# Down projection of a decoder block: another order of the seven products, sums of weights made with their operand, six entries ahead

## The chip, the cores and the metric

One core of a Trainium2 chip runs the whole block in one launch. The metric is device microseconds from start to end of an execution; several executions are timed and the median is given. Another execution is recorded by the hardware profiler; its events are what "the profile" and "the trace" mean below.

## The reference

A decoder block on x of shape (1, 1024, 1024), float32: two mixers (a chunkwise mLSTM with four heads, and a causal pooling over four windows), gated and merged into the residual, then a SwiGLU feed-forward layer with 2816 hidden features and a last normalization. The change touches the final lines alone:

```python
x = x + (g_a * y_a + g_b * y_b) @ w_out[l]
h2 = rms_norm(x, norm2_g[l])
x = x + (jax.nn.silu(h2 @ w_ffn_gate[l]) * (h2 @ w_ffn_up[l])) @ w_ffn_down[l]
return rms_norm(x, final_norm_g)
```

## The kernel before

Everything is kept with features on partitions and tokens along a row. A float32 operand is split into a high and a low fp32r half (`split`, L130: ScalarE casts the high half, L131, and VectorE subtracts for the low one, L132), and a product of two such operands is three matmuls (`mm3`, L143 to L145). Large products use a scheme with seven half-size products instead of eight; the seven are named in `OPS` (b11, d1, d2, b21, d3, b22, d4), after the right-hand operand. The left operand of each is a block of weights or a sum of blocks.

The feed-forward stage makes the hidden features two tiles at a time (`hidden`, L840) and writes the seven right-hand operands of each of the 11 pairs to memory (`stage`, L834, DMA at L838, tensor `tg_d`). The names `fd`, `s` are its own operands, `e` its results.

The down stage (from L887) multiplies them with `w_down`. The 11 pairs are cut into three chunks of 4, 3 and 4 pairs. The work is a list of **entries** (L941): for each chunk c, each step s (one of the seven products), each of the four pairs of output rows q. One entry is a product over the chunk's pairs: 12 (or 9) matmuls of 128x512. TensorE gets the entries in this order, as the scheduler allows. Four pools lie at the right end of on-chip memory: `s1p` (sums of weights), `rbp` (second half of the raw weights), `tgp` (right-hand tiles `tg`, 13 places), `ap` (left operands `a`, 6 places). A pool that opens where another has closed lies over its tiles, and a load into it waits until those were last read.

The steps are in the same order in all chunks:

```python
STEPS = ("b21", "d1", "b22", "b11", "d2", "d3", "d4")
```

`down_lefts` (L903) is a generator for one (c, q): each `next` makes the left operand of the next step. At d1 it makes all sums of the weights at once (L920 to L924). `make_ready` (L943) draws the operand of the entry `EARLY` = 4 places ahead. `down_rights` (L935) issues on SP the `tg` loads of the next step when a step begins. `down_weights` (L896) loads raw weights: those of the next chunk at steps b22 (first halves) and d3 (second halves). Ahead of the loop SP gets the first weights, the `tg` of step one, the `rb` halves, the eight residual tiles `x` (L970), then the `tg` of step two.

A product is added to the residual by VectorE (L1037). b22 goes on in d1's PSUM bank (`C`), and d2, d3, d4 go on in b11's (`A`). PSUM has six banks `mm` and two `aux`.

In the last chunk the final normalization runs beside the products: `square` (L976) adds up squares, `scaled` (L984) applies the gain to the first 512 tokens, `turn` (L988) transposes those back to token rows, and `later_tokens` (L997) finishes the other 512 tokens: sums by token (L280), the power on POOL (L261), the factors spread along rows (L272 to L274), eight scalings on VectorE (L1004), eight stores. It is called after d3's last entry. The loop breaks off at the last entry (d4, q = 3), which is done in two halves of 256 tokens in the tail (L1057 to L1089), each followed by its mean (L1073), its power (L1074), transposes (L1077), scalings (L1086, L1088) and stores (L1089).

Of the kernel before, what the change touches and what calls it, by code (L numbers as in the profile page):

```python
# [47 lines left out]
EARLY = 4  # L48
# [18 lines left out]
def tile_hybrid_block(ctx, tc, x, xt, consts, params, w_fm, w_v, w_pool, w_a, w_b, w_out, w_gate, w_up, w_down, out, out_rows):  # L67
# [704 lines left out]
    with ExitStack() as c5:  # L772
# [116 lines left out]
        s1p = pool(c7, "s1p", KH, "right")  # L889
        rbp = pool(c7, "rbp", KH, "right")  # L890
        tgp = pool(c7, "tgp", 13, "right")
        ap = pool(c7, "ap", 6, "right")
        STEPS = ("b21", "d1", "b22", "b11", "d2", "d3", "d4")
        raws, lefts, rights, todo = {}, {}, {}, []
# [8 lines left out]
        def down_lefts(c, q):  # L903

            a11, a12 = raws[c, q, 0]
            n = a11.shape[-1]

            def tile_():
                t = ap.tile([P, 2, 512], F32R, tag="a", name="a")
                return t[:, :, :n]  # L910

            def op(src):
                t = tile_()
                operand(t, src)
                return t

            yield op(a12)
            a21, a22 = raws[c, q, 1]
            s1 = s1p.tile([P, 512], F32, tag="s1", name="s1")[:, :n]
            nc.vector.tensor_add(out=s1, in0=a21, in1=a22)  # L920
            t = op(s1)
            nc.vector.tensor_sub(out=a21, in0=a11, in1=a21)
            nc.vector.tensor_sub(out=s1, in0=s1, in1=a11)
            nc.vector.tensor_sub(out=a12, in0=a12, in1=s1)  # L924
            yield t
            yield op(a12)
            yield op(a11)
            yield op(s1)
            yield op(a21)
            t = tile_()  # L930
            nc.scalar.activation(out=t[:, 0, :], in_=a22, func=AF.Copy, scale=-1.0)
            nc.vector.scalar_tensor_tensor(out=t[:, 1, :], in0=a22, scalar=-1.0, in1=t[:, 0, :].bitcast(F32), op0=ALU.mult, op1=ALU.subtract)
            yield t

        def down_rights(c, s):  # L935
            for i in range(*CHUNKS[c]):
                t = tgp.tile([P, 2, 512], F32R, tag="tg", name="tg")
                nc.sync.dma_start(out=t.bitcast(F32), in_=tg_d[i, OPS.index(STEPS[s])].rearrange("p (a n) -> p a n", a=2))
                rights.setdefault((c, s), []).append(t)

        entries = [(c, s, q) for c in range(len(CHUNKS)) for s in range(len(STEPS)) for q in range(KH)]  # L941

        def make_ready(e):  # L943
            if e >= len(entries):
                return
            c, s, q = entries[e]
            if s == 0:
                lefts[c, q] = down_lefts(c, q)
            todo.append(next(lefts[c, q]))
# [23 lines left out]
    LAST = KT - 1  # L973
# [37 lines left out]
    A, C = [None] * KH, [None] * KH  # L1011
    whole = slice(0, 512)
    for e, (c, s, q) in enumerate(entries):
        final = c == len(CHUNKS) - 1
        if q == 0:
            if s + 1 < len(STEPS):
# [4 lines left out]
        if s == 2 and not final:  # L1021
            down_weights(c + 1, q, 0)
        if s == 5 and not final:
            down_weights(c + 1, q, 1)
        a, ts = todo.pop(0), rights[c, s]
        (o10, o11), (o20, o21) = halves(x3[q]), halves(x3[q + KH])
        if final and s == 6 and q == KH - 1:
            break
        if s == 0:
            ps = bank()  # L1030
        elif s in (1, 2):
            ps = C[q] = bank() if s == 1 else C[q]
        else:
            ps = A[q] = bank() if s == 3 else A[q]
        product(ps, a, ts, whole, s in (0, 1, 3), True)
        o = (o10, o21, o11, o10, o11, o21, o20)[s]
        nc.vector.tensor_add(out=o, in0=ps, in1=o)  # L1037
        if not final:
            continue
        if s == 3:  # L1040
            square(q, 0)
            scaled(q)
        if s == 4:
            square(q, 1)
            if q == 1:
                for t in range(4):
                    turn(t, 0, KH)
        if s == 5:
            square(q + KH, 1)
            if q == KH - 1:  # L1050

# [98 lines left out]
```

## Time and profile before

| what | value |
|---|---|
| median of 3 runs | 1507.25 us (1505.81 to 1508.13) |
| the profiled execution itself | 1509.98 us |
| its span in the trace | 1508.3 us |
| mean granted clock of TensorE | 0.99 of full speed |
| busy share of the span: TensorE, VectorE, ScalarE | 98%, 75%, 48% |
| bytes moved by DMA | 262.18 MB, mean 174 GB/s |
| down stage, from its first to its last product | 1267.5 to about 1489 us |

The span is what the trace shows; the execution's own time is a little longer. Busy shares are averages over stages with different limits, so the stretches around the change are read one by one. PE is TensorE, PEld its weight loads, DVE VectorE, ACT ScalarE, SP the engine that issues most DMAs (SPq is its DMA queue).

### The profile page before, as it was taken

Reading aid. Unit: us, or ns where it says so; the run is one execution under the profiler, and the core shown is the slowest. Engines: PE = TensorE matmul, PEld = TensorE weight load, DVE = VectorE, ACT = ScalarE, POOL = GpSimd, SP = SyncE. Lnnn points to the kernel's source line nnn. Section 1 sums busy time; section 2 is a strip of 40 time slices with the busy share of each in tenths; the row PEclk is TensorE's granted clock in tenths of the full one; section 3 lists DMA queues with packets and bytes.
Section 4 is the critical chain, followed back from the end, with each engine's and each line's share of the span. In section 5 each row is a group of like instructions: output and inputs, shape, how many; then the busy total and the mean of one; then the engine's idle time right before and its main releaser. Section 6 shows DMA issues by size and latency. Waiting matters only on the chain.

```text
span 1508.3 us, 19546 instructions
## 1 busy us (share of the span) xinstructions
PE 1480.2 (98%) x7051; PEld 1249.0 (83%) x7051; DVE 1130.9 (75%) x2033; ACT 729.3 (48%) x1327; POOL 28.5 (2%) x58
## 2 busy tenths in 40 slices
PE   9999999999999999999999999999999998899996
PEld 9998888878887789998888788888888887788885
DVE  5757878797877678766567779888888876666765
ACT  6475655556543478862233455444444442222243
POOL 0000000000000011110000000000000000000000
PEclk9999999999999999999999999999999999899998
DMA  6662433233333598728343326434444446966633
GB/s 204 198 248 86 151 126 126 98 140 112 140 105 119 176 314 290 247 78 303 129 127 124 105 82 232 168 140 155 156 150 154 158 150 258 407 246 250 240 148 112
DMA packets 101296, 262.18 MB, mean 174 GB/s; under 512 B 9804, under 2 KB 45772, under 8 KB 101200
## 3 DMA queue, kind: packets, MB, share of 16 engines
q1 hardware_dynamic: 86032, 221.09, 42.0%
q10 hardware_dynamic: 15168, 39.85, 7.0%
q8 instruction: 55, 0.90, 0.3%
q14 instruction: 41, 0.34, 0.1%
HBM read 172.29 MB, written 88.62 MB: 173 GB/s over the span
## 4 chain that ended last, share of the span: by engine, by line
PE 95%; DVE 2%; DMA 1%; issue 1%; ACT 0%; SPq 0%; POOLq 0%; POOL 0%; ACTq 0%; DVEq 0%
PE mm L143 26%; PE mm L145 26%; PE mm L144 26%; PE mm L155 14%; DMA v<-v_d 1%; PE aux L683 0%; PE mm L524 0%; DMA yb<-yb_d 0%; DVE x L1004 0%; PE aux L573 0%; DMA o<-in_xt 0%; DVE a L132 0%; PE aux L280 0%; PE mm L993 0%; PE aux L143 0%
## 5 line engine op out<-in xcount | busy, mean ns | idle before, releaser
L131 ACT CAST s<-raw 128x512 fp32r<-128x512 f32 x220 | 133.6, 621 | 194.4 <-PE mm L145 158.7
L132 DVE TENSOR_TENSOR s<-raw,s 128x512 fp32r<-128x512 f32 x220 | 148.6, 686 | 29.6 <-ACT s L131 29.0
L143 PE MATMUL mm<-fd,s 128*128 128x512 f32 x352 | 137.6, 392 | 3.0 <-ACT e L226 2.2
L143 PE MATMUL mm<-zd,s 128*128 128x512 f32 x352 | 137.6, 393 | 0.3 <-DVE o L234 0.3
L144 PE MATMUL mm<-fd,s 128*128 128x512 f32 x352 | 137.6, 391 | 0.0
L145 PE MATMUL mm<-fd,s 128*128 128x512 f32 x352 | 137.5, 391 | 0.0
L145 PE MATMUL mm<-zd,s 128*128 128x512 f32 x352 | 137.5, 391 | 0.0
L144 PE MATMUL mm<-zd,s 128*128 128x512 f32 x352 | 137.3, 390 | 0.0
L143 PE MATMUL mm<-tg,a 128*128 128x512 f32 (+1 forms) x312 | 122.3, 392 | 7.4 <-ACT a L131 7.4
L144 PE MATMUL mm<-tg,a 128*128 128x512 f32 (+1 forms) x312 | 121.7, 390 | 0.0
L145 PE MATMUL mm<-tg,a 128*128 128x512 f32 (+1 forms) x312 | 121.6, 390 | 0.0
L1037 DVE TENSOR_TENSOR x<-mm,x 128x512 f32<-128x512 f32 x83 | 57.2, 689 | 63.0 <-PE mm L145 62.9
L143 PE MATMUL mm<-zb,s 128*128 128x512 f32 x264 | 104.0, 395 | 0.0
L143 PE MATMUL mm<-fb,s 128*128 128x512 f32 x264 | 103.0, 391 | 0.0
L144 PE MATMUL mm<-fb,s 128*128 128x512 f32 x264 | 103.0, 390 | 0.0
L144 PE MATMUL mm<-zb,s 128*128 128x512 f32 x264 | 102.9, 390 | 0.0
L145 PE MATMUL mm<-zb,s 128*128 128x512 f32 x264 | 102.9, 390 | 0.0
L145 PE MATMUL mm<-fb,s 128*128 128x512 f32 x264 | 102.7, 390 | 0.0
L143 PEld LDWEIGHTS mm<-fd,s 128*128 128x128 f32 x352 | 66.3, 188 | 17.8 <-ACT e L226 2.9
L143 PEld LDWEIGHTS mm<-zd,s 128*128 128x128 f32 x352 | 66.1, 188 | 14.7 <-DVE o L234 0.8
L145 PEld LDWEIGHTS mm<-fd,s 128*128 128x128 f32 x352 | 66.4, 189 | 13.9
L144 PEld LDWEIGHTS mm<-zd,s 128*128 128x128 f32 x352 | 66.1, 188 | 14.1 <-issue 0.5
(330 smaller groups left out, 3445.3 us busy)
## 6 DMA issues: line engine op xcount, KB each, us to landing
tg_d<-t SPq DMA_DIRECT2D x77, 512.0 KB, 3.4
tg<-tg_d SPq DMA_DIRECT2D x77, 512.0 KB, 6.0
raw<-in_w_fm SPq DMA_DIRECT2D x44, 512.0 KB, 3.7
z_d<-o ACTq DMA_DIRECT2D x24, 512.0 KB, 2.9
raw<-in_w_gate SPq DMA_DIRECT2D x22, 512.0 KB, 3.7
raw<-in_w_up SPq DMA_DIRECT2D x22, 512.0 KB, 4.6
q_d<-x ACTq DMA_DIRECT2D x16, 512.0 KB, 2.7
rc<-z_d SPq DMA_DIRECT2D x32, 256.0 KB, 5.2
```

What stands on the lines that cost most here:

```text
L131: hi_made = nc.scalar.copy(out=hi, in_=src)
L132: split.last = hi_made.ins, nc.vector.tensor_sub(out=lo, in0=src, in1=hi.bitcast(F32)).ins
L143: nc.tensor.matmul(out, lhsT=l[0], rhs=r[0], start=start, stop=False, skip_group_check=resume)
L144: nc.tensor.matmul(out, lhsT=l[0], rhs=r[1], start=False, stop=False, skip_group_check=resume)
L145: mm3.last = nc.tensor.matmul(out, lhsT=l[1], rhs=r[0], start=False, stop=stop, skip_group_check=resume)
L155: nc.tensor.matmul(ps[half], lhsT=l[a], rhs=r[half][b], start=(k == 0 and (a, b) == (0, 0)), stop=(k == nk - 1 and a == 1),)
L1037: nc.vector.tensor_add(out=o, in0=ps, in1=o)
```

## The change

- `EARLY` is 6 instead of 4, `ap` has 8 places instead of 6, `tgp` 11 instead of 13; a pool `s4p` of two tiles is new, and the pools stand in another order (`tgp` ahead of `rbp`).
- The steps are b21, b11, d1, b22, d2, d3, d4 in the first two chunks; in the last chunk b21 comes last.
- `down_left` makes the operand of one entry with the sum that it needs: a21+a22 at d1, that less a11 and a12 less the result at b22, a11-a21 at d3. a12 is no longer overwritten.
- d1 and b22 have a bank each, `aux` for odd q and `mm` for even; d1's product is added in two places.
- Both halves of the next chunk's weights are loaded at d3.
- `later_tokens` still follows d3's last entry, which now is eight entries ahead of the end instead of four, since d4 and b21 follow it. The first 512 tokens of the rows 4 to 7 are turned at b21, q = 1; those of the rows 0 to 3 in the tail. The last entry is b21, q = 3, and the tail stores the columns from 512 on first.

```diff
 NPAIR = NFF // 2
 CHUNKS = ((0, 4), (4, 7), (7, 11))
 
-EARLY = 4
+EARLY = 6
 
 
 C_ID, C_TRI, C_ONE, C_INV = 0, 128, 256, 384
...
         c7 = ctx.enter_context(ExitStack())
         del places[0]
         s1p = pool(c7, "s1p", KH, "right")
+        s4p = pool(c7, "s4p", 2, "right")
+        tgp = pool(c7, "tgp", 11, "right")
         rbp = pool(c7, "rbp", KH, "right")
-        tgp = pool(c7, "tgp", 13, "right")
-        ap = pool(c7, "ap", 6, "right")
-        STEPS = ("b21", "d1", "b22", "b11", "d2", "d3", "d4")
-        raws, lefts, rights, todo = {}, {}, {}, []
+        ap = pool(c7, "ap", EARLY + 2, "right")
+
+        STEPS = [("b21", "b11", "d1", "b22", "d2", "d3", "d4")] * 2 + [("b11", "d1", "b22", "d2", "d3", "d4", "b21")]
+        raws, sums, rights, todo = {}, {}, {}, []
 
         def down_weights(c, q, fh):
             k0, k1 = CHUNKS[c]
...
             nc.sync.dma_start(out=t[:, :2 * n], in_=w_down[q, fh, :, 2 * k0 * P:2 * k1 * P])
             raws[c, q, fh] = t[:, :n], t[:, n:2 * n]
 
-        def down_lefts(c, q):
-
-            a11, a12 = raws[c, q, 0]
+        def down_left(c, s, q):
+
+            (a11, a12), (a21, a22) = (raws[c, q, fh] for fh in range(2))
             n = a11.shape[-1]
-
-            def tile_():
-                t = ap.tile([P, 2, 512], F32R, tag="a", name="a")
-                return t[:, :, :n]
-
-            def op(src):
-                t = tile_()
-                operand(t, src)
+            b = STEPS[c][s]
+            t = ap.tile([P, 2, 512], F32R, tag="a", name="a")[:, :, :n]
+            if b == "d4":
+                nc.scalar.activation(out=t[:, 0, :], in_=a22, func=AF.Copy, scale=-1.0)
+                nc.vector.scalar_tensor_tensor(out=t[:, 1, :], in0=a22, scalar=-1.0, in1=t[:, 0, :].bitcast(F32), op0=ALU.mult, op1=ALU.subtract)
                 return t
-
-            yield op(a12)
-            a21, a22 = raws[c, q, 1]
-            s1 = s1p.tile([P, 512], F32, tag="s1", name="s1")[:, :n]
-            nc.vector.tensor_add(out=s1, in0=a21, in1=a22)
-            t = op(s1)
-            nc.vector.tensor_sub(out=a21, in0=a11, in1=a21)
-            nc.vector.tensor_sub(out=s1, in0=s1, in1=a11)
-            nc.vector.tensor_sub(out=a12, in0=a12, in1=s1)
-            yield t
-            yield op(a12)
-            yield op(a11)
-            yield op(s1)
-            yield op(a21)
-            t = tile_()
-            nc.scalar.activation(out=t[:, 0, :], in_=a22, func=AF.Copy, scale=-1.0)
-            nc.vector.scalar_tensor_tensor(out=t[:, 1, :], in0=a22, scalar=-1.0, in1=t[:, 0, :].bitcast(F32), op0=ALU.mult, op1=ALU.subtract)
-            yield t
+            if b == "d1":
+                s1 = sums[c, q] = s1p.tile([P, 512], F32, tag="s1", name="s1")[:, :n]
+                nc.vector.tensor_add(out=s1, in0=a21, in1=a22)
+            elif b == "b22":
+                s1 = sums[c, q]
+                nc.vector.tensor_sub(out=s1, in0=s1, in1=a11)
+                s4 = s4p.tile([P, 512], F32, tag="s4", name="s4")[:, :n]
+                nc.vector.tensor_sub(out=s4, in0=a12, in1=s1)
+            elif b == "d3":
+                nc.vector.tensor_sub(out=a21, in0=a11, in1=a21)
+            operand(t, {"b21": a12, "b11": a11, "d1": sums.get((c, q)), "b22": b == "b22" and s4, "d2": sums.get((c, q)), "d3": a21}[b])
+            return t
 
         def down_rights(c, s):
             for i in range(*CHUNKS[c]):
                 t = tgp.tile([P, 2, 512], F32R, tag="tg", name="tg")
-                nc.sync.dma_start(out=t.bitcast(F32), in_=tg_d[i, OPS.index(STEPS[s])].rearrange("p (a n) -> p a n", a=2))
+                nc.sync.dma_start(out=t.bitcast(F32), in_=tg_d[i, OPS.index(STEPS[c][s])].rearrange("p (a n) -> p a n", a=2))
                 rights.setdefault((c, s), []).append(t)
 
-        entries = [(c, s, q) for c in range(len(CHUNKS)) for s in range(len(STEPS)) for q in range(KH)]
+        entries = [(c, s, q) for c in range(len(CHUNKS)) for s in range(len(OPS)) for q in range(KH)]
 
         def make_ready(e):
             if e >= len(entries):
                 return
-            c, s, q = entries[e]
-            if s == 0:
-                lefts[c, q] = down_lefts(c, q)
-            todo.append(next(lefts[c, q]))
+            todo.append(down_left(*entries[e]))
 
         early_made = []
         for q in range(KH):
...
         nc.sync.dma_start(out=t, in_=x2_d[j])
         x3.append(t)
     rows = [op.tile([P, D], F32, tag="o", name="o") for _ in range(4)]
-    LAST = KT - 1
+    LAST = KH - 1
     acc = [None, None]
 
     def square(j, half):
...
         for kp, t in enumerate(ts):
             mm3(ps, [a[:, i, kp * P:(kp + 1) * P] for i in range(2)], [t[:, i, sl] for i in range(2)], start and kp == 0, stop and kp == len(ts) - 1, True)
 
-    A, C = [None] * KH, [None] * KH
+    A = [None] * KH
     whole = slice(0, 512)
     for e, (c, s, q) in enumerate(entries):
         final = c == len(CHUNKS) - 1
         if q == 0:
-            if s + 1 < len(STEPS):
+            if s + 1 < len(OPS):
                 down_rights(c, s + 1)
             elif not final:
                 down_rights(c + 1, 0)
         make_ready(e + EARLY)
-        if s == 2 and not final:
-            down_weights(c + 1, q, 0)
-        if s == 5 and not final:
-            down_weights(c + 1, q, 1)
+        b = STEPS[c][s]
+        if b == "d3" and not final:
+            for fh in range(2):
+                down_weights(c + 1, q, fh)
         a, ts = todo.pop(0), rights[c, s]
         (o10, o11), (o20, o21) = halves(x3[q]), halves(x3[q + KH])
-        if final and s == 6 and q == KH - 1:
+        if final and b == "b21" and q == KH - 1:
             break
-        if s == 0:
-            ps = bank()
-        elif s in (1, 2):
-            ps = C[q] = bank() if s == 1 else C[q]
+        if b in ("b21", "d1", "b22"):
+            ps = bank("aux" if q % 2 else "mm")
         else:
-            ps = A[q] = bank() if s == 3 else A[q]
-        product(ps, a, ts, whole, s in (0, 1, 3), True)
-        o = (o10, o21, o11, o10, o11, o21, o20)[s]
-        nc.vector.tensor_add(out=o, in0=ps, in1=o)
+            ps = A[q] = bank() if b == "b11" else A[q]
+        product(ps, a, ts, whole, b in ("b21", "b11", "d1", "b22"), True)
+        for o in {"b21": [o10], "b11": [o10], "d1": [o21, o11], "b22": [o11], "d2": [o11], "d3": [o21], "d4": [o20]}[b]:
+            nc.vector.tensor_add(out=o, in0=ps, in1=o)
         if not final:
             continue
-        if s == 3:
+        if b == "d2":
+            square(q, 1)
+        if b == "d3":
+            square(q + KH, 1)
+            if q == KH - 1:
+                later_tokens()
+        if b == "d4":
+            square(q + KH, 0)
+            scaled(q + KH)
+        if b == "b21":
             square(q, 0)
             scaled(q)
-        if s == 4:
-            square(q, 1)
             if q == 1:
                 for t in range(4):
-                    turn(t, 0, KH)
-        if s == 5:
-            square(q + KH, 1)
-            if q == KH - 1:
-
-                nc.vector.tensor_add(out=o20, in0=ps, in1=o20)
-                later_tokens()
-        if s == 6:
-            square(q + KH, 0)
-            scaled(q + KH)
-    r, left, right = o20, a, ts
+                    turn(t, KH, KT)
+    r, left, right = o10, a, ts
     sq = sqd.tile([P, 512], F32, tag="sq1", name="sq")
     ms = sm.tile([P, 4], F32, tag="ms", name="ms")
     rs = sm.tile([P, 4], F32, tag="rs", name="rs3")
...
         product(ps, left, right, sl, True, True)
         if p == 0:
             for t in range(4):
-                turn(t, KH, LAST)
+                turn(t, 0, LAST)
             nc.vector.tensor_scalar(out=ms, in0=token_sums(acc[0], 4), scalar1=1.0 / D, scalar2=EPS, op0=ALU.mult, op1=ALU.add)
         nc.vector.tensor_add(out=r[:, sl], in0=ps, in1=r[:, sl])
         nc.scalar.activation(out=sq[:, sl], in_=r[:, sl], func=AF.Square)
...
         ps = bank("aux")
         for i in range(2):
             nc.tensor.transpose(out=ps[:, i * P:(i + 1) * P], in_=r[:, (2 * p + i) * P:(2 * p + i + 1) * P], identity=ident)
-        for c0, c1 in ((0, 512), (512, D)):
+        for c0, c1 in ((512, D), (0, 512)):
             for i in range(2):
                 t = 2 * p + i
-                sources = [(c0, min(c1, LAST * P), rows[t])] + [(LAST * P, D, ps)] * (c1 == D)
+                sources = [(c0, c1, rows[t])] if c0 else [(c0, LAST * P, rows[t]), (LAST * P, c1, ps)]
                 for a, b, src in sources:
                     o = rows[t][:, a:b]
                     src = ps[:, i * P:(i + 1) * P] if src is ps else o
```

The new line numbers that matter: `tg` loads L931, weight loads L902, `x` loads L960, additions L1025, squares L969 and L971, turned rows L983 and L985, the later tokens' scalings L994, tail L1055 to L1075.

The first place where the order moves is SP at the start of the down stage: from the first `tg` load of b21 to the first of the eight `x` loads. The names in brackets are the semaphores that an issue waits for (DMAHW: an earlier transfer, PE: TensorE). Before:

```order
L938 DMA tg<-tg_d 128x1024 [waits DMAHW0_49,PE_49]
L938 DMA tg<-tg_d 128x1024 [waits DMAHW1_49,PE_49]
L938 DMA tg<-tg_d 128x1024 [waits DMAHW2_49]
L938 DMA tg<-tg_d 128x1024 [waits DMAHW3_49,PE_49]
L900 DMA rb<-in_w_down 128x1024 [waits DMAHW4_49]
L900 DMA rb<-in_w_down 128x1024 [waits DMAHW5_49,PE_49]
L900 DMA rb<-in_w_down 128x1024 [waits DMAHW6_49]
L900 DMA rb<-in_w_down 128x1024 [waits DMAHW7_49]
L970 DMA x_11342<-x_d 128x1024 [waits DMAHW0_49]
```

With the change:

```order
L931 DMA tg<-tg_d 128x1024 [waits DMAHW0_49,PE_49]
L931 DMA tg<-tg_d 128x1024 [waits DMAHW1_49,PE_49]
L931 DMA tg<-tg_d 128x1024 [waits DMAHW2_49]
L931 DMA tg<-tg_d 128x1024 [waits DMAHW3_49]
L902 DMA rb<-in_w_down 128x1024 [waits DMAHW4_49]
L902 DMA rb<-in_w_down 128x1024 [waits DMAHW5_49]
L902 DMA rb<-in_w_down 128x1024 [waits DMAHW6_49]
L902 DMA rb<-in_w_down 128x1024 [waits DMAHW7_49]
L960 DMA x_11351<-x_d 128x1024 [waits DMAHW0_49]
```

The loads stand in the same order; the fourth `tg` and the second `rb` no longer wait for TensorE, the first and the second `tg` still do. Seven more `x` loads and then the `tg` of step two follow in both.

The second place is VectorE behind the additions of the last products (`x_…` are residual tiles, `rsb` the later tokens' factors, `o` the turned rows). Before:

```order
L1070 TENSOR_TENSOR x_11356<-mm,x_11356 128x256
L1069 TENSOR_SCALAR ms<-aux 128x4
L1072 TENSOR_SCALAR x_11356<-x_11356,par 128x256
L995 COPY o<-mm 128x384 x2
L1004 SCALAR_TENSOR_TENSOR x_11342<-x_11342,par,rsb 128x512
L1004 SCALAR_TENSOR_TENSOR x_11344<-x_11344,par,rsb 128x512
```

With the change:

```order
L994 SCALAR_TENSOR_TENSOR x_11363<-x_11363,par,rsb 128x512
L994 SCALAR_TENSOR_TENSOR x_11365<-x_11365,par,rsb 128x512
L985 COPY o<-mm 128x512
L971 TENSOR_TENSOR sq<-sq 128x512
L985 COPY o<-mm 128x512
L1025 TENSOR_TENSOR x_11355<-mm,x_11355 128x512
L1056 TENSOR_TENSOR x_11357<-mm,x_11357 128x256
```

Before, the eight scalings stood behind the last addition of all; now they stand ahead of the copies of turned rows, of the third product's addition (L1025) and of the last product's two (L1056).

## Rows read from the trace of the kernel before

**Rows 1.** The page, chain that ended last: shares of the span by engine

```profile
PE 95%; DVE 2%; DMA 1%; issue 1%; ACT 0%; SPq 0%; POOLq 0%; POOL 0%; ACTq 0%; DVEq 0%
```

**Rows 2.** Waits of PE from 1100 us: who waited, for whom; total, times, longest us

```profile
PE mm L143 <- ACT a L131: 7.4, 1, 7.4
```

**Rows 3.** Windows: us, busy of PE, PEld, DVE, ACT, POOL; PEclk, DMA share, GB/s

```profile
1280.00:1284.00 4.00, 0.00 (x0) 0.00 (x0) 4.00 (x8) 0.62 (x1) 0.00 (x0) 0.68 1.03 410
1284.00:1288.00 4.00, 2.06 (x5) 1.70 (x6) 4.00 (x8) 0.62 (x1) 0.00 (x0) 0.50 1.00 365
1288.00:1292.00 4.00, 4.00 (x11) 3.09 (x11) 1.95 (x4) 0.62 (x1) 0.00 (x0) 0.54 1.03 421
```

**Rows 4.** Timeline around the gap: start, duration in us, instruction, [idle before, releaser]

```profile
1265.87 0.39 PE L145 MATMUL mm<-fd,s 128*128 128x512 f32 x1
...
1266.55 0.39 PE L145 MATMUL mm<-fd,s 128*128 128x512 f32 x1
...
1275.52 0.68 DVE L132 TENSOR_TENSOR a<-s,a 128x512 fp32r<-128x512 f32 x1
...
1285.94 0.77 PE L143 MATMUL mm<-tg,a 128*128 128x512 f32 x1 [7.44 <-ACT a L131]
```

**Rows 5.** Timeline of SP's DMA issues at the start of the down stage

```profile
1258.65 4.84 SPq L938 DMA_DIRECT2D tg<-tg_d  x4
1263.55 4.71 SPq L900 DMA_DIRECT2D rb<-in_w_down  x4
1268.31 6.33 SPq L970 DMA_DIRECT2D x<-x_d  x8
1275.60 2.88 SPq L938 DMA_DIRECT2D tg<-tg_d  x3
```

**Rows 6.** DMA issues at 1267.83 and at 1275.60: count, KB, us to landing

```profile
rb<-in_w_down SPq DMA_DIRECT2D x1, 512.0 KB, 6.5
...
tg<-tg_d SPq DMA_DIRECT2D x1, 512.0 KB, 10.2
```

**Rows 7.** Timeline of SP, one step's tiles loaded with nothing else under way

```profile
1420.16 2.36 SPq L938 DMA_DIRECT2D tg<-tg_d  x4
```

**Rows 8.** DMA issues of that step: the first, and the fourth at 1422.20

```profile
tg<-tg_d SPq DMA_DIRECT2D x1, 512.0 KB, 3.2
...
tg<-tg_d SPq DMA_DIRECT2D x1, 512.0 KB, 6.3
```

**Rows 9.** Timeline of the tail, from 1481 us to the last power

```profile
1481.00 0.39 PE L143 MATMUL mm<-tg,a 128*128 128x512 f32 x1
...
1484.86 0.95 PE L280 MATMUL aux<-cst,sq 128*128 128x1 f32 x8
...
1487.38 0.28 PE L143 MATMUL mm<-tg,a 128*128 128x256 f32 x1
...
1492.66 0.58 ACT L274 COPY rsb<-aux 128x512 f32<-128x512 f32 x1 [0.48 <-PE aux L273]
...
1493.71 5.38 DVE L1004 SCALAR_TENSOR_TENSOR x<-x,par,rsb 128x512 f32<-128x512 f32 x8
...
1501.18 0.69 POOL L1074 TENSOR_TENSOR rs<-ms,nhalf 128x2 f32<-128x2 f32 x1 [1.25 <-DVE ms L1073]
```

**Rows 10.** Timeline of PE: eight transposes and the matmul behind them

```profile
1460.10 1.04 PE L993 MATMUL mm<-cst,x 128*128 128x128 f32 x8
1460.89 0.49 PE L143 MATMUL mm<-tg,a 128*128 128x512 f32 x1
```

**Rows 11.** Windows, columns as in 3: an idle stretch and what followed

```profile
851.00:853.00 2.00, 0.12 (x1) 0.00 (x0) 2.00 (x4) 1.09 (x3) 0.00 (x0) 1.00 0.00 0
855.00:858.00 3.00, 3.00 (x9) 2.33 (x8) 1.57 (x4) 0.75 (x2) 0.00 (x0) 0.50 1.00 376
```

**Rows 12.** Windows and lines of DVE: the full stretch

```profile
1290.00:1480.00 190.00, 190.00 (x844) 157.42 (x843) 122.20 (x198) 56.41 (x95) 0.00 (x0) 1.00 0.64 240
...
L1037 DVE TENSOR_TENSOR x<-mm,x 128x512 f32<-128x512 f32 x76 | 52.4, 690 | 60.2 <-PE mm L145 60.2
```

## The prediction

> **What bounds the kernel now.** I read the shares of the chain of waits first: TensorE carries 95% of the chain that ends last [rows 1], so an edit counts only where it moves a stretch in which TensorE stands still, or work that stands on TensorE. The waits of TensorE from 1100 us on come next: one of 7.4 us, before a matmul of the down stage [rows 2]. From 1290 to 1480 us TensorE is busy 190.00 of 190.00 us with 844 matmuls [rows 12], so a product of twelve matmuls takes 12 × 0.225 = 2.7 us there. That leaves three places for this change: the gap at the start of the down stage, the work that it puts on or takes off the full stretch, and the tail behind 1481 us.
>
> **The gap, and who really ends it.** b21 of chunk 0 ends at 1278.5 us, and d1 starts at 1285.94 [rows 4]. The profile puts the 7.44 us down to a ScalarE cast. That cast is not it: the low half of d1's first operand was finished by VectorE at 1275.52 + 0.68 = 1276.2 us [rows 4]. What landed last is the first tile of d1's right side: issued at 1275.60 [rows 5], 10.2 us to landing [rows 6], so 1285.8. It stood in line. SP issues four `tg`, four `rb`, eight `x` tiles and only then this one [rows 5]. The fourth `rb` (issued at 1267.83, 6.5 us [rows 6]) landed at 1274.3, and from there nine transfers of 512 KB took 11.5 us: 1.28 us each, with the DMA engines' share at 1.0 and 365 to 421 GB/s [rows 3]. The gap is a transfer limit, and it also brings the granted clock down: 0.68 in 1280 to 1284, 0.50 in 1284 to 1288, 0.54 in 1288 to 1292 [rows 3], about 5.7 us of work at the lower level (1.2 GHz), worth 2.8 us.
>
> By row the rate is 410 GB/s. The Trainium skill ("Perfetto Trace Analysis", Roofline) gives 358 GB/s as a core's share of memory and about 435 GB/s as what the 16 DMA engines of a single active core reach. As an estimate by that page a tile would cost 1.46 or 1.2 us, and the next part's term +5.2 or +4.1 us; the measured row decides.
>
> **Part 1, the new pools at the start.** Step two is now b11 instead of d1, but SP's order is the same: its tiles stand behind `tg` ×4, `rb` ×4, `x` ×8. So neither the six entries ahead nor the later sums (VectorE work) can close the gap: cost and gain nothing, covered by the queue of transfers. What does change is where the tiles lie. In the built order, before, the second and fourth `tg` and the second `rb` wait for TensorE; now the second `tg` does, and no `rb`. By the new places of the pools the second `tg` lies over the second of the four right-hand tiles of the last FFN product (d4), so it waits for that product's sixth matmul, which ends at 1265.87 + 0.39 = 1266.3 us [rows 4]. Before, all four `tg` were issued by 1263.5 [rows 5], and the `rb` that waited (for the same product's third tile, ninth matmul) could go at 1266.55 + 0.39 = 1266.9 [rows 4]. All 15 issues behind the second `tg`, up to b11's first tile, are queued behind that wait. At 1266.3 sixteen transfers are then to do (3 `tg`, 4 `rb`, 8 `x`, b11's first). From an idle start the nearest row is the step whose tiles were issued from 1420.16 on [rows 7]: the first took 3.2 us and the fourth, issued at 1422.20, 6.3 [rows 8], so the fourth lands 8.3 us after the first issue. 1266.3 + 8.3 + 12 × 1.28 = 1290.0 against 1285.8: **+4.2 us**. Bounds: if all after the first land at the full rate, 1266.3 + 3.2 + 15 × 1.28 = 1288.7 (+2.9); by counting that four transfers fewer are done (5.1 us) and the queue restarts 0.7 us earlier than at the `rb`, +4.4. I take the middle one since it uses the start-up as it was seen. b21 itself starts on time: its second tile lands by 1271 at the latest by the same rows, and is wanted about 1270, so up to 1 us of this may be lost earlier and is then hidden in the same gap. The half-clock stretch behind the gap stays as long as it is: 0.
>
> **Part 2, the full stretch.** Products: 84 before and after, 0. Added: twelve DVE additions (d1 into two places), 12 × 0.69 = 8.3 us [rows 12], and one less of that length (the extra addition at the end); VectorE is busy 122.2 of 190 us there [rows 12] and each bank is asked for again four entries (11 us) later, so 0; uncovered it would be TensorE waiting for a bank, at most the 8.3. `tgp` with 11 tiles instead of 13: the fourth tile of a step takes the place of a tile freed a whole step (11 us) before it is wanted, so 0; what that costs without cover is a rival below. The weight loads of the next chunk move to d3 together, behind the tiles of d4 on SP: hidden by a step of slack.
>
> **Part 3, what changes sides around E.** Call E the moment when TensorE is done with the first of the last step's four products: 1481.00, where the second begins [rows 9]. Before, two groups of eight transposes stood ahead of E, the first from 1460.10 with the next matmul at 1460.89 and that one 0.1 us longer [rows 10]: 0.9 us each. They now stand behind it: −1.8. Eight matmuls of sums by token, 0.95 us [rows 9], move ahead of it with `later_tokens`: +1.0. Together **−0.8 us**.
>
> **Part 4, the tail from E.** Before: 1508.3 − 1481.0 = 27.3 us, in which VectorE did eight scalings, 5.38 us from 1493.71 [rows 9], between the last addition and the second half's mean. They now start earlier, but not early enough. They need the ScalarE copy of the row (at 1492.66, 0.58 us, before [rows 9]), whose last matmul stands behind the second product after E: 0.4 + 2.7 + 0.3 + 0.2 + 0.6 = 4.2 us after E. Eight scalings: to 9.6. In VectorE's new order the copies of two turned rows, a sum of squares and the third product's addition come behind them, 4 × 0.6: to 12.0. TensorE's second half product needs the bank which that addition frees, so it runs from 12.1 to 13.5 (1.4, the half products of [rows 9]) though TensorE had been done at about 9.1 + 1.0: a new wait of about 2 us. Then addition and square to 15.1, the power on POOL 0.7 [rows 9], scalings to 17.2, the second mean (about 0.2) and power to 18.1, and 1508.3 − 1501.87 = 6.4 us from there to the end [rows 9]: 24.5. An idle TensorE of 2.5 us at 851 us was followed by a granted clock of 0.50 at 855 to 858 [rows 11]; 0.5 us for that: 25.0. So 25.0 − 27.3 = **−2.3 us**; bounds −0.5 (the copies later than I count, each step on a slower clock) and −4.5 (the scalings never hold TensorE up).
>
> **Sum:** +4.2 − 0.8 − 2.3 = **+1.1 us** on the profiled execution (1509.98). That one lies 2.7 us above the median shown, and I move the median by the same: 1507.25 + 1.1 = **1508.4**. Ends of the terms: +2.9 − 0.8 − 4.5 = −2.4 and +4.4 − 0.8 − 0.5 = +3.1, so 1504.9 to 1510.4 for this case.
>
> **The rivals.**
> *The gap closes.* If the wait were on the operand, as the profile names it, six entries ahead would remove 7.4 us, the 2.8 of clock and the 3.1 of parts 3 and 4: 1507.25 − 13.3 = 1494. For it: the releaser in [rows 2]. Against: the operand at 1276.2 and transfers without a break [rows 3, 4]. 0.06.
> *The scalings do not hold TensorE* (ScalarE's copy sooner, or the addition ahead in time): 4.2 − 0.8 − 4.5 = −1.1, 1506. It decides by whether the third product's addition ends before about 10 us after E. 0.15. With the gap at its lower end it is 1504.9.
> *A second gap (slower).* Eleven `tg` places make SP wait at a tile that is still read, with staging writes and weight loads queued behind it; the next steps' tiles in chunk 0 come late. It decides from a delay of 6 us on, roughly the slack of a step against four transfers at 1.28 (10.8 − 5.1). Price: 3 us of waiting and 2.8 of half clock again as in [rows 3], about +6: 1507.25 + 1.1 + 6 = 1514.3. For it: SP already runs without a break there [rows 5]; against: 240 GB/s from 1290 on [rows 12]. 0.13.
> *The change does less than it says* at the start (the wait at the second `tg` passes early): 0 − 0.8 − 2.3, 1504.2. 0.06.
>
> **How the numbers follow.** Forecast 0.60, the rivals as given. A measurement of this kernel can tell about 0.2%, 3.0 us, from no change. Faster by more than that (below 1504.2): the closed gap, and half of the last rival with a little of the second, 0.12. Slower by more (above 1510.3): the second gap, and the forecast's upper edge with 0.08, 0.21. The rest, 0.67, within. The range 1504.0 to 1512.0 leaves out the closed gap and the second gap, together about 0.19.
>
> **What would show it.** Right: the second `tg` on SP at about 1266.3, b11's first matmul near 1290, no other TensorE wait before 1480, VectorE's eight scalings ahead of a 2 us wait of TensorE, E to the end 25 us. Wrong: b11 starting by 1283, a wait of over 2 us between 1292 and 1480, or a tail under 23 us.

## The result, and the profile after

The changed kernel takes 1509.8 us (median of 20 runs, 1506.91 to 1512.53) against 1507.95 us before (20 runs, 1505.41 to 1509.77): a ratio of 1.0013, 95% interval 1.0007 to 1.0019. That is 1.9 us longer, where 1.1 had been forecast.

The profiled execution of the changed kernel is one of its fast ones: 1507.59 us, span 1505.9. By spans alone the change would seem 2.4 us *faster* than before (1508.3), so the two traces are compared stretch by stretch. The last product of the feed-forward stage, which nothing in the change touches, starts 2.2 us earlier than in the trace of before (1262.40 against 1264.60), and everything behind it is shifted by that. In the ten traces of the experiments it starts between 1262.59 and 1263.94, those of the old kernel (1262.59 and 1263.78) among the others. Before and after:

```profile
1264.60 0.50 PE L143 MATMUL mm<-fd,s 128*128 128x512 f32 x1 [0.78 <-DVE e L234]
...
1262.40 0.50 PE L143 MATMUL mm<-fd,s 128*128 128x512 f32 x1 [0.78 <-DVE e L234]
```

The three longest waits of TensorE from 1100 us on, after the change (columns as in [rows 2]):

```profile
PE mm L143 <- DMA tg<-tg_d: 12.2, 1, 12.2
PE mm L983 <- DVE o L985: 1.3, 2, 0.8
PE aux L1063 <- DVE ms L1059: 1.3, 1, 1.3
```

The gap at the start of the down stage is 12.2 us instead of 7.4 [rows 2], and now the profile names its releaser rightly, a `tg` tile. The issues on SP, which answer to [rows 5], and behind them, by itself, the second of the first four `tg`:

```profile
1256.44 8.91 SPq L931 DMA_DIRECT2D tg<-tg_d  x4
1265.40 1.99 SPq L902 DMA_DIRECT2D rb<-in_w_down  x4
1267.44 9.74 SPq L960 DMA_DIRECT2D x<-x_d  x8
1278.18 11.89 SPq L931 DMA_DIRECT2D tg<-tg_d  x10
...
1264.09 0.32 SPq L931 DMA_DIRECT2D tg<-tg_d  x1
```

TensorE's timeline at the two ends of that wait, and at the point E of the prediction, which answers to [rows 4, 9]:

```profile
1263.66 0.39 PE L145 MATMUL mm<-fd,s 128*128 128x512 f32 x1
...
1288.54 0.76 PE L143 MATMUL mm<-tg,a 128*128 128x512 f32 x1 [12.23 <-DMA tg<-tg_d]
...
1481.39 0.38 PE L983 MATMUL mm<-cst,x 128*128 128x128 f32 x2
...
1493.51 0.39 PE L143 MATMUL mm<-tg,a 128*128 128x256 f32 x1 [0.16 <-DVE x L1025]
```

The second `tg` is issued at 1264.09, when the sixth matmul of the last product ends (1263.66 + 0.39 = 1264.05). The rest of the queue goes behind it. Windows of the changed kernel (columns as in [rows 3]):

```profile
1280.00:1284.00 4.00, 0.00 (x0) 0.00 (x0) 4.00 (x8) 0.45 (x1) 0.00 (x0) 0.65 1.03 410
1284.00:1288.00 4.00, 0.00 (x0) 0.00 (x0) 4.00 (x7) 0.00 (x0) 0.00 (x0) 0.50 1.03 410
1288.00:1292.00 4.00, 3.46 (x9) 2.83 (x10) 0.73 (x2) 0.00 (x0) 0.00 (x0) 0.57 1.03 410
1291.00:1478.00 187.00, 187.00 (x830) 154.97 (x829) 124.38 (x205) 52.20 (x92) 1.01 (x1) 1.00 0.68 246
```

The transfers run without a break through the gap (410 GB/s), and from 1291 us TensorE is busy 187.00 of 187.00 us, so there is no second gap. In the tail the eight scalings are where the order put them, ahead of the copies and the third addition (VectorE's timeline):

```profile
1485.67 5.39 DVE L994 SCALAR_TENSOR_TENSOR x<-x,par,rsb 128x512 f32<-128x512 f32 x8 [0.16 <-ACT rsb L274]
1490.98 0.68 DVE L985 COPY o<-mm 128x512 f32<-128x512 f32 x1
1491.58 0.68 DVE L971 TENSOR_TENSOR sq<-sq 128x512 f32<-128x512 f32 x1
1492.18 0.68 DVE L985 COPY o<-mm 128x512 f32<-128x512 f32 x1
1492.78 0.68 DVE L1025 TENSOR_TENSOR x<-mm,x 128x512 f32<-128x512 f32 x1
```

Stretch by stretch against the profiled execution of before:

| stretch | before | after | difference |
|---|---|---|---|
| start to the last feed-forward product | 1264.60 | 1262.40 | −2.2 (not the change's) |
| wait ahead of step two | 7.44 | 12.23 | +4.8 |
| step two's first matmul to E | 195.06 | 192.85 | −2.2 |
| E to the end of the span | 27.3 | 24.5 | −2.8 |

Without the first line the sum is −0.2 us, while the medians differ by +1.9. The section on the reasons comes back to these 2 us.

### The profile page after: what moved, and what is told of

Its sections match the earlier page's. It is cut to its first block, busy times and chain, and to the rows that moved or that the text cites. A ratio compares the mean times of both kernels' runs of the same rounds, so it can differ in the third digit from the quotient of the medians.

```text
span 1505.9 us, 19563 instructions
## 1 busy us (share of the span) xinstructions
PE 1477.0 (98%) x7051; PEld 1245.8 (83%) x7051; DVE 1136.3 (75%) x2044; ACT 727.9 (48%) x1327; POOL 28.7 (2%) x58
## 4 chain that ended last, share of the span: by engine, by line
PE 94%; DMA 3%; DVE 2%; ACT 0%; SPq 0%; issue 0%; POOLq 0%; POOL 0%; ACTq 0%
PE mm L143 25%; PE mm L145 25%; PE mm L144 25%; PE mm L155 13%; PE aux L144 1%; PE aux L143 1%; PE aux L145 1%; DMA x<-x_d 1%; DMA tg<-tg_d 1%; DMA v<-v_d 1%; PE mm L524 0%; PE aux L683 0%; DMA yb<-yb_d 0%; DMA rc<-z_d 0%; DVE x L994 0%
## 5 line engine op out<-in xcount | busy, mean ns | idle before, releaser
L143 PE MATMUL mm<-tg,a 128*128 128x512 f32 (+1 forms) x250 | 97.3, 390 | 12.4 <-DMA tg<-tg_d 12.2
L144 PE MATMUL mm<-tg,a 128*128 128x512 f32 (+1 forms) x250 | 97.1, 388 | 0.0
L145 PE MATMUL mm<-tg,a 128*128 128x512 f32 (+1 forms) x250 | 97.0, 389 | 0.0
L1025 DVE TENSOR_TENSOR x<-mm,x 128x512 f32<-128x512 f32 x72 | 49.1, 688 | 48.5 <-PE mm L145 48.5
L143 PEld LDWEIGHTS mm<-fd,s 128*128 128x128 f32 x352 | 66.5, 189 | 17.8 <-ACT e L226 2.9
L143 PEld LDWEIGHTS mm<-zd,s 128*128 128x128 f32 x352 | 66.1, 188 | 14.7 <-DVE o L234 0.8
L145 PEld LDWEIGHTS mm<-fd,s 128*128 128x128 f32 x352 | 66.5, 189 | 13.9
L144 PEld LDWEIGHTS mm<-fd,s 128*128 128x128 f32 x352 | 66.5, 189 | 13.8
```

The source lines that it names most:

```text
L143: nc.tensor.matmul(out, lhsT=l[0], rhs=r[0], start=start, stop=False, skip_group_check=resume)
L144: nc.tensor.matmul(out, lhsT=l[0], rhs=r[1], start=False, stop=False, skip_group_check=resume)
L145: mm3.last = nc.tensor.matmul(out, lhsT=l[1], rhs=r[0], start=False, stop=stop, skip_group_check=resume)
```

## The experiments

Theory: the gap is the queue of transfers, and it grew because the second `tg` waits longer; the tail is held by VectorE's scalings. Rivals: operands, or VectorE, make the gap; the tail is held by something else.

**1. The old order of the pools.** Only the places of the pools change back; the waits of the first eight loads are then those of before.

```diff
         s1p = pool(c7, "s1p", KH, "right")
-        s4p = pool(c7, "s4p", 2, "right")
-        tgp = pool(c7, "tgp", 11, "right")
         rbp = pool(c7, "rbp", KH, "right")
+        tgp = pool(c7, "tgp", 11, "right")
+        s4p = pool(c7, "s4p", 2, "right")
         ap = pool(c7, "ap", EARLY + 2, "right")
```

> The changed kernel with its pools in the old order (s1p, rbp, tgp with 11, s4p, ap), nothing else. Then the second tg load no longer waits for the sixth matmul of the last FFN product, and the second rb load waits for its ninth, as before the change. Theory (the late second tg holds the whole queue of transfers): the gap ahead of b11 falls from 12.2 to about 7.4 us, the median by 4.8 us to about 1505.0, ratio to before 0.998. Rival (the gap is long because operands of b11 and d1 are made in another order by a full VectorE): the gap stays at 12 us, the median at 1509.8, ratio 1.001.

Measured: 1506.26 us, ratio 0.9982 (0.9972 to 0.9991). The waits of TensorE:

```profile
PE mm L143 <- DMA tg<-tg_d: 7.8, 1, 7.8
```

The gap is back at 7.8 us and the ratio is 0.0031 lower than the change's, 4.7 us. With nearly equal gaps the rest of the change is a gain of 2.7 us (1.4 to 4.2 by the interval).

**2. The kernel before with the late second `tg`.** The opposite edit: the pools of before placed like those of the change.

```diff
-        rbp = pool(c7, "rbp", KH, "right")
-        tgp = pool(c7, "tgp", 13, "right")
+        s4p = pool(c7, "s4p", 2, "right")
+        tgp = pool(c7, "tgp", 12, "right")
+        rbp = pool(c7, "rbp", KH, "right")
```

> The kernel before, with only its pools placed like those of the change (two unused tiles, tgp of 12 ahead of rbp): its second tg load then waits for the ninth matmul of the last FFN product instead of an earlier one. Theory (that wait alone makes the gap longer): the gap ahead of d1 goes from 7.4 to 12 to 13 us, the median from 1508 to 1512.5 or 1513.5, ratio 1.003 to 1.004. Rival (the longer gap of the change comes from its other order of steps and operands): the gap stays within 1 us of 7.4, ratio 1.000.

Measured: 1514.14 us, ratio 1.0030 (1.0019 to 1.0040). The first matmul of d1:

```profile
1290.78 0.76 PE L143 MATMUL mm<-tg,a 128*128 128x512 f32 x1 [12.60 <-DMA tg<-tg_d]
```

12.6 us with the old steps, the old operands and four entries ahead. So the places of the pools alone make the longer gap, in either kernel, and are worth 0.3% each way.

**3. Step two's tiles ahead of the residual tiles.**

```diff
+    down_rights(0, 1)
     for j in range(KT):
         t = x3p.tile([P, S], F32, tag="x3", name="x3")
         nc.sync.dma_start(out=t, in_=x2_d[j])
...
-        if q == 0:
+        if q == 0 and e > 0:
             if s + 1 < len(OPS):
                 down_rights(c, s + 1)
```

> The changed kernel with the four tg loads of step two (b11) issued ahead of the eight x loads instead of behind them. Theory (the gap is the queue of transfers at 1.28 us each): b11's first tile lands 8 x 1.28 = 10.2 us sooner, the gap ahead of b11 falls from 12.2 to about 2 us; d1's tiles still stand behind the x loads, so a second wait of about 4.5 us comes ahead of d1; together -5.8 us and up to 1.5 less of low clock: median 1502.5 to 1504, ratio 0.997. Rival (the wait is on operands, as the profile of before named it): gap stays at 10 us or more, median 1508 to 1510.

Measured: 1503.96 us, ratio 0.9965 (0.9952 to 0.9977). TensorE's two waits:

```profile
1278.30 0.47 PE L143 MATMUL mm<-tg,a 128*128 128x512 f32 x1 [1.47 <-DMA tg<-tg_d]
1293.65 0.77 PE L143 MATMUL mm<-tg,a 128*128 128x512 f32 x1 [4.19 <-DMA tg<-tg_d]
```

1.5 and 4.2 us where 2 and 4.5 were expected. Nothing but the order of twelve transfers moved, so the transfers are the wait.

**4. All transfers by need.**

```diff
         down_rights(0, 0)
+        down_rights(0, 1)
         for q in range(KH):
             down_weights(0, q, 1)
...
     for j in range(KT):
+        if j == KH:
+            down_rights(0, 2)
         t = x3p.tile([P, S], F32, tag="x3", name="x3")
...
-        if q == 0:
+        if q == 0 and e > KH:
```

> The changed kernel with the transfers at the start of the down stage in the order in which they are needed: tg of b21, tg of b11, rb, x 0 to 3, tg of d1, x 4 to 7. Theory (queue of transfers alone): no wait of TensorE over 1 us ahead of b11 and at most 1 us ahead of d1, no fall of the clock: -12.2 + 1 - 1.5 = about -12.5 us, median 1497 (1495 to 1499), ratio 0.993. Rival (VectorE, busy without a break from 1276 to 1286 us, is the next limit): operands of d1 or the first additions come late, 4 to 6 us of waiting stay, median 1501 to 1504.

Measured: 1499.47 us, ratio 0.9937 (0.9924 to 0.9949), between the theory's 1495 to 1499 and the rival's 1501 to 1504. What is left of the waits at the start:

```profile
PE mm L143 <- DMA tg<-tg_d: 1.5, 1, 1.5
PE mm L143 <- ACT a L131: 1.2, 1, 1.2
```

Ahead of b11 nothing of 12.2 us is left; in d1 there are two shorter waits. The first is for a tile. The second is put down to an operand's cast on ScalarE, but that is not it:

```profile
1292.81 0.19 PEld L143 LDWEIGHTS mm<-tg,a 128*128 128x128 f32 x1 [1.55 <-ACT a L131]
...
1292.20 0.62 ACT L131 CAST a<-s 128x512 fp32r<-128x512 f32 x1 [4.87 <-DVE s L922]
...
1292.02 0.68 DVE L1028 TENSOR_TENSOR x<-mm,x 128x512 f32<-128x512 f32 x1
```

The weights were already loading at 1292.81, while the cast ran to 1292.82 (and its input came from L922, the sum for b22). What ended just before is an addition of VectorE, at 1292.70; by these times it is the likely cause, and the expectation's rival, VectorE, has a share of 1.2 us.

**5. The same in the kernel before.** Old steps, with `tg` of b21, `rb`, `tg` of d1, `x` 0 to 3, `tg` of b22, `x` 4 to 7.

```diff
         for q in range(KH):
             down_weights(0, q, 1)
+        down_rights(0, 1)
...
     for j in range(KT):
+        if j == KH:
+            down_rights(0, 2)
         t = x3p.tile([P, S], F32, tag="x3", name="x3")
...
-        if q == 0:
+        if q == 0 and e > KH:
```

> The kernel before, old steps and all, with its transfers at the start in the order of need: tg of b21, rb, tg of d1, x 0 to 3, tg of b22, x 4 to 7. Theory (transfers made the gap, and behind them stands VectorE, which makes all sums of weights at d1): d1's first tile lands at 1275.6, so the 7.4 us go, but the operands of the later entries of d1 come when VectorE has made them (the third one's at about 1281.6 us, the fourth's at 1284 in the trace of before): a wait of 1 to 3 us on operands stays, median 1508.5 - 5.5 - 2 (clock) = 1501 (1499 to 1503), ratio 0.995. Rival (transfers alone): no wait over 1 us, median 1498, ratio 0.993. Other rival (the profile's releaser was right all along, an operand): 1507 to 1508.5.

Measured: 1505.66 us, ratio 0.9984 (0.9975 to 0.9993): 0.16% where the like edit brings 0.76% to the change (which had 4.8 us more of gap to lose), and less than was expected. The waits, and VectorE's timeline where they end:

```profile
PE mm L143 <- ACT t L131: 2.7, 1, 2.7
PE mm L143 <- DVE x L1040: 2.0, 1, 2.0
```

```profile
1283.13 0.68 DVE L1040 TENSOR_TENSOR x<-mm,x 128x512 f32<-128x512 f32 x1
...
1292.03 0.69 DVE L132 TENSOR_TENSOR a<-raw,a 128x512 fp32r<-128x512 f32 x1 [2.42 <-ACT a L131]
1292.64 0.68 DVE L132 TENSOR_TENSOR t<-e,t 128x512 fp32r<-128x512 f32 x1
1293.24 0.68 DVE L1040 TENSOR_TENSOR x<-mm,x 128x512 f32<-128x512 f32 x1
...
1296.29 1.47 DVE L1040 TENSOR_TENSOR x<-mm,x 128x512 f32<-128x512 f32 x2 [0.57 <-DMA x<-x_d]
```

No `tg` tile stops TensorE any more, but 4.7 us of new waits came, and what ends both is an addition of VectorE and not, as I had thought, an operand of the waiting product. The first (to 1283.96) is for a bank whose addition stands behind the sums of weights, on a VectorE that is busy 16.00 of 16.00 us from 1272 to 1288. The second (to 1294.03) ends with the addition at 1293.24 + 0.68, and not with the cast `t` that the profile names: b22 goes on in d1's bank `C`, so it waits until d1's product has been added. That addition stands on VectorE behind the operand of a later entry, for whose cast VectorE sat idle for 2.42 us.

The order is also not quite by need here. In the old kernel d1 is added to the residual tiles 4 to 7, which this edit loads last. The first of them was issued at 1279.94; as an estimate by the 11.2 us of the tile issued just ahead of it, it landed at about 1291.1. So transfers alone would have held that addition back until then, but not until 1293.24; the last of the four additions waits for its tile in the row above.

Later sums, a bank each for d1 and b22, and more places for operands are parts of the change, and all bear on these two waits. That they pay once the transfers stand in the right order is likely by the two runs together, but it is not shown: none was tried alone.

**6. Four entries ahead.**

```diff
-EARLY = 6
+EARLY = 4
...
-        ap = pool(c7, "ap", EARLY + 2, "right")
+        ap = pool(c7, "ap", EARLY + 4, "right")
```

> The changed kernel with operands made four entries ahead instead of six, ap still with eight places, nothing else. Theory (no operand is waited for anywhere in the stretch): gap of 12 us as it is, no new wait of TensorE before 1470 us, median 1509.8 within 1 us, ratio 1.001. Rival (the two more entries ahead pay for the later sums): waits on operands at the start of steps, 3 us or more longer, ratio 1.003 and over.

Measured: 1511.81 us, ratio 1.0019 (1.0010 to 1.0028); the interval overlaps the change's own. The gap is 11.9 us and no wait of TensorE is new before 1470 us; the one new row is in the tail:

```profile
PE mm L983 <- DVE o L985: 2.2, 1, 2.2
```

The look-ahead of six does nothing for the start. Whether the tail's order costs the 0.0006 is not settled.

**7. Scalings split, first try.** Four of the eight were called in the tail instead (`later_scaled(KH, KT)` behind the first half's multiplication).

> The changed kernel with four of the eight scalings of the later tokens moved behind the first half of the last product. Theory (the block of eight scalings on VectorE holds the third addition and with it TensorE): the second half product starts about 2 us sooner, the tail from the last step's second product to the end is 22.4 instead of 24.5 us, median 1507.7, ratio 0.9998. Rival (the moved scalings delay the second half's mean as they did before the change): no gain or up to 1 us longer, median 1509.8 to 1511.

Measured: 1508.48 us, ratio 1.0003 (0.9995 to 1.0012). A miss: seven scalings still stood ahead. The place of the call does not fix the place of the instruction; the scheduler moved one of the four.

```profile
1488.34 4.73 DVE L997 SCALAR_TENSOR_TENSOR x<-x,par,rsb 128x512 f32<-128x512 f32 x7 [0.16 <-ACT rsb L274]
```

**8. Three scalings held to the end**, by an ordering constraint on VectorE's last multiplication (`ended`); the other five stay where they were.

```diff
...
+    with tc.issue_after(ended.ins):
+        later_scaled(5, KT)
```

> The changed kernel with three of the eight scalings of the later tokens held back, by an ordering constraint, until VectorE's last other instruction (the edit before this one moved only one scaling, and that behind a copy). Theory (the block on VectorE holds the third addition, and that holds TensorE's last half product): three scalings of 0.66 us less ahead of it, the second half product starts 10.1 instead of 12.1 us after the first product of the last step, the tail is 22.5 instead of 24.5 us, median about 1507.8, ratio 0.9998. Rival (TensorE is held by the copies of turned rows and not by the scalings): it starts at 12 us as it does now, median 1509.8 or above.

Measured: 1509.1 us, ratio 0.9999 (0.9990 to 1.0008); the expected median was 1507.8, the expected ratio 0.9998. The mechanism is the one expected: the second half product starts 1491.70 − 1481.57 = 10.1 us after E, where the change has 12.1.

```profile
1491.70 0.38 PE L143 MATMUL mm<-tg,a 128*128 128x256 f32 x1
```

But this profile's tail is 1506.1 − 1481.57 = 24.5 us, as before. The stores tell why:

```profile
1496.27 4.46 SPq L1078 DMA_DIRECT2D out<-o  x8
1500.82 1.98 SPq L998 DMA_DIRECT2D out<-x  x3
```

Three stores now stand behind the last eight, 2.0 us: what TensorE gained, the end of the queue took.

**9. All three together**: experiments 4, 1 and 8 (in the expectation the third, the first and the fifth run).

> The changed kernel with the transfers by need as in the third run, the old order of the pools as in the first, and three scalings held back as in the fifth. Theory: the second tg goes 5 us earlier, so the 1.5 us ahead of d1 that the third run kept are gone; the operand's 1.2 us may stay; the tail is 2 us shorter: 1499.5 - 1.5 - 2.0 = 1496.0 (1494 to 1498), ratio 0.992 of before. Rival (VectorE is now the limit at the start, and TensorE's clock the limit in the tail): 1498 to 1500, no better than the third run.

Measured: 1494.49 us, ratio 0.9901 (0.9887 to 0.9914). No wait is left at the start of the down stage; the two longest stand elsewhere, in the tail and ahead of the last feed-forward product:

```profile
PE aux L1069 <- DVE ms L1065: 1.3, 1, 1.3
PE mm L143 <- DVE e L234: 0.8, 1, 0.8
```

That is better by 1.5 us than expected, with no gain in the tail (24.6 us from E): the old places of the pools let the queue start earlier, and all of b11, `rb` and d1 land ahead of need.

**10. Copies on ScalarE**: experiments 4 and 1, all scalings at their place, the turned rows' four copies on ScalarE.

```diff
-        copy = nc.scalar.copy if t % 2 else nc.vector.tensor_copy
+        copy = nc.scalar.copy if t % 2 or j0 else nc.vector.tensor_copy
```

> The last run's start (transfers by need, old order of the pools), all eight scalings where the change has them, and the four copies of the rows turned at b21, q = 1 on ScalarE instead of two of them on VectorE. Theory (what VectorE has ahead of the third addition holds TensorE; ScalarE has nothing to do there for 5.6 us; the stores at the end are not lengthened this time): the third addition ends 1.2 us sooner and the transposes no longer wait for VectorE's copies, the second half product starts 10.3 to 10.9 us after the last step's first product instead of 12.1, the tail is 22.7 to 23.3 instead of 24.6 us: median 1493.0 (1492.5 to 1493.8), ratio 0.989. Rival (the eight stores at the end set the time, not TensorE): 1494.5 as in the last run.

Measured: 1494.32 us, ratio 0.9903 (0.9889 to 0.9916). The second half product starts where expected, 1479.75 − 1468.83 = 10.9 us after E, and this profile's tail is 23.3 us, as expected; but the median was expected at 1493.0, is where the rival had it (1494.5), and cannot be told from experiment 9 (four runs each). So the gain in the tail is seen in one execution and not shown in the time.

```profile
1479.75 0.38 PE L143 MATMUL mm<-tg,a 128*128 128x256 f32 x1 [0.71 <-DVE x L1028]
```

Both of the last two are about 1% faster than either kernel of the case.

## Why the prediction was right

**The gap, +4.2 forecast, +4.8 measured.** The cause is shown from both sides (experiments 1 and 2) and the queue by experiments 3 and 4. The size is beyond the upper bound given (+4.4). From the second `tg` to the landing of b11's first tile the sum had 8.3 + 12 × 1.28 = 23.7 us; measured are 1278.18 + 10.2 − 1264.09 = 24.3. The issues at 1265.40 (the first `rb`), 1266.96 (the fourth) and 1278.18 (b11's first tile):

```profile
rb<-in_w_down SPq DMA_DIRECT2D x1, 512.0 KB, 6.9
...
rb<-in_w_down SPq DMA_DIRECT2D x1, 512.0 KB, 9.9
...
tg<-tg_d SPq DMA_DIRECT2D x1, 512.0 KB, 10.2
```

The start-up was as forecast: the fourth transfer, the first `rb`, landed at 1272.3, 8.2 us after the second `tg` was issued (forecast 8.3). The 0.6 us lie behind it: the next three `rb` took until 1276.9, 4.6 us, where the sum counted 3 × 1.28 = 3.8. From there nine transfers took 11.5 us, 1.28 us each, the 410 GB/s of the row. Why the three took longer is open. Neither of the two rates of the Trainium skill ("Perfetto Trace Analysis", Roofline) that the prediction weighed against the row was needed: the measured one lies between them.

**The low clock behind the gap, 0 forecast, about −1.4 measured in this pair.** Before, TensorE ran at the lower level for some 5.7 us after it restarted [rows 3]; after, for some 2.9 us, from 1288.54 to about 1291.5. Windows of 1 us at both ends of the low stretch, before and after:

```profile
1281.00:1282.00 1.00, 0.00 (x0) 0.00 (x0) 1.00 (x3) 0.00 (x0) 0.00 (x0) 0.72 1.06 422
1291.00:1292.00 1.00, 1.00 (x4) 0.77 (x4) 0.53 (x1) 0.44 (x1) 0.00 (x0) 0.66 1.01 414
...
1281.00:1282.00 1.00, 0.00 (x0) 0.00 (x0) 1.00 (x2) 0.00 (x0) 0.00 (x0) 0.61 1.02 406
1291.00:1292.00 1.00, 1.00 (x5) 0.82 (x4) 0.00 (x0) 0.00 (x0) 0.00 (x0) 0.77 1.01 401
```

With 0.50 between them, the low stretch runs from 1281.4 to 1291.7 before and from 1281.2 to 1291.5 after: it is as long in both, and the longer gap has used up more of it. In experiment 2, with a restart at 1290.78, it lasted from 1283.2 to 1296.9, with 6.1 us of it behind the restart:

```profile
1292.00:1296.00 4.00, 4.00 (x10) 3.07 (x10) 0.69 (x1) 0.62 (x1) 0.00 (x0) 0.50 1.03 419
1296.00:1297.00 1.00, 1.00 (x4) 0.77 (x3) 0.00 (x0) 0.00 (x0) 0.00 (x0) 0.56 1.00 410
```

So the step "stays as long as it is" failed. What a gap of 11.8 to 12.6 us leaves of the low stretch is between 2.9 and 6.1 us in the kept traces (the change, experiments 2, 6, 7 and 8), and at half the clock that is a difference of 1.6 us, about as much as a term of the sum.

**Around E, −0.8 forecast.** From the restart to E the trace shows −2.2; less the −1.4 of the clock that is −0.8. No second gap came, and the twelve added additions and `tgp` of 11 cost TensorE nothing (187.00 of 187.00 us).

**The tail, −2.3 forecast, −2.8 in this profile.** The step on which it rested is there to a tenth: the second half product starts 1493.51 − 1481.39 = 12.1 us after E. The 0.5 us that I had added for the clock was not spent in this execution. (The idle stretch at 851 us that it was taken from was 2.2 us long, not 2.5.) In experiment 1, with the same instructions in the tail, the granted clock fell to 0.50 and the tail from E took 1505.6 − 1479.02 = 26.6 us:

```profile
1492.00:1494.00 2.00, 2.00 (x12) 2.00 (x11) 1.02 (x3) 0.66 (x2) 0.00 (x0) 0.50 0.00 0
1494.00:1496.00 2.00, 2.00 (x11) 2.00 (x12) 0.56 (x3) 0.42 (x1) 0.00 (x0) 0.50 0.00 0
```

The same tail took 24.4 us in experiment 3 and 24.8 in experiment 4, and the old one 27.3 in all three traces of the old kernel (before, experiments 2 and 5). So the new tail is 2.5 to 2.9 us shorter in three traces and 0.7 in one. The forecast's −2.3, with 0.5 us for the clock, lies between: in the kept traces the clock costs there either next to nothing or about 2 us.

**The sum.** The medians can be split by experiment 1: the places of the pools cost 4.7 us (0.0031; 0.0030 in experiment 2), and the rest of the change brings 2.7. The forecast had +4.2 and −3.1 for these two, so each half came out within 0.5 us of its forecast, less than these runs can tell, and the sum is not right by two errors that cancel. The two profiles, without the first line of the table, have −0.2 us where the medians have +1.9: the clock of the one profile of the change was kind at both places. The 20 runs of the change go from 1506.91 us at a mean granted clock of 0.994 to 1512.53 at 0.990, and 0.001 of 1508 us is 1.5 us. That the 2 us between profiles and medians are the clock's, in these two stretches, fits the numbers; no run separates it.

**The rivals.** The closed gap on account of operands: refuted by experiment 3, and the look-ahead does nothing for it (experiment 6). A second gap from fewer `tg` places: it did not come. Scalings that do not hold TensorE: refuted by the 12.1 us and experiment 8. A wait that passes early: refuted by the 1264.09.

## What to carry to other kernels

Ask of a wait in the profile what landed or ended last, not what is named: in the kernel before, the operand was ready nine microseconds before the tile, and in experiments 4 and 5 a cast was named where, by the times, an addition ended the wait. Where a transfer queue sets the start of a stage, look at the order of its transfers first: here it was worth 0.76%, and the look-ahead in compute nothing that the runs show. A pool's new place can put a wait at its head that every transfer behind it pays (here 0.3%). Compare two traces stretch by stretch, since the spans of two single executions can differ the other way than the medians do.

## What was not expected of the hardware

After a like idle stretch TensorE worked at the lower clock for between 2.9 and 6.1 us (restart at 1288.54 in the change, at 1290.78 in experiment 2), and the same 2 us of waiting in the tail were followed by a fall of the clock in one execution (0.50 from 1492 us on, experiment 1) and not in another (1.00 to about 1499 us, the change). The 20 runs of the change spread over 5.6 us, those of before over 4.4.
